# A hybrid decoder layer with a PEER mixer: 96 gathered tokens instead of 64, and the last 32 dense tokens in 32-column strips

## The chip, the cores and the metric

The kernel runs on one core of one Trainium2 chip. The metric is device time in microseconds (us) of one execution, the median of the runs shown; for the kernel before that is 888.08 us (three runs, 887.66 to 889.19). The profile is one execution, recorded by the hardware profiler.

## What is computed

A decoder layer on 256 tokens of width 1024: a mixing part (gated linear attention beside block-sparse attention, one input and one output projection) and then a mixer that looks experts up. Only the mixer is touched by the change. There are 16384 experts, each a row of `peer_u` and a row of `peer_v`; every token picks 128 of them (8 heads, 16 each) by product keys:

```python
    q = (xt @ w_query).reshape(T, PEER_HEADS, 2, PEER_QDIM // 2)
    s = jnp.einsum('thpd,hpkd->thpk', q, subkeys).astype(jnp.float32)
    sv, si = lax.top_k(s, PEER_TOPK)
    ...
    top_s, pos = lax.top_k(cand, PEER_TOPK)
    expert = jnp.take_along_axis(cand_id, pos, axis=-1)
    gate = jax.nn.softmax(top_s, axis=-1)
    ...
        ug = u_tab[ec]
        vg = v_tab[ec]
        act = jax.nn.gelu(jnp.einsum('thkd,td->thk', ug, xc).astype(jnp.float32), approximate=False)
        w = (gc * act).astype(vg.dtype)
        return jnp.einsum('thk,thkd->td', w, vg)
```

## The kernel before

**Two ways for the tokens.** The first `NS` = 64 tokens fetch the rows of their own experts from HBM: a gather (L725, an indirect DMA that GpSimd issues) brings 128 rows of 4 KB, one for each partition. Two partitions serve one token, so 64 gathers of `u_rows` and 64 of `v_rows` cover 64 tokens with 128 experts each. `few_u` (L728) multiplies and sums a gathered tile against the tokens' rows, `few_v` (L737, L740) adds a gathered row, scaled by its gate, into a running sum; both are VectorE instructions over 1024 columns. The gathers have five buffers (L720).

The other `ND` = 192 tokens are computed densely, against all 16384 experts. The *up-projection* (loop at L801, 64 steps `jp` of two 512 KB pieces of `u`) multiplies each piece, in eight f32 matmuls (L112, `by_col_whole`), with the 192 tokens as the moving columns, and applies Gelu. In its second half one-hot matrices of the selected experts (L771, L772, L775) are multiplied in groups of four tokens (L786, 48 groups of eight matmuls) into a grid of gates, which is multiplied into the activations. The *down-projection* (loop at L863) has 128 columns `j` of experts, one 512 KB piece of `v` each. ScalarE and VectorE split the piece (L92, L93) and the weights `W` (L873, L874) into a high and a low part of reduced f32 ("f32r"), so that a product is three f32r matmuls (`mm3`, L68 to L70) instead of one f32 matmul. The result is summed in PSUM over all 128 columns: `prod_a` (L850) for dense tokens 0 to 127, six matmuls of 512 columns for each `j`; `prod_x` (L855) for the other 64, whose high and low weights lie side by side as 128 columns, four matmuls (L859) for each `j`. At the end `few_sum` (L848) and L890 fold partial sums with f32 matmuls of 64 weight columns, L894 adds the residual and L896 stores. In the profile an f32 matmul is two instructions, each with its own weight load; an f32r matmul is one.

**What sets the order.** The program is built with a scheduler (L960, `schedule_with_timeline_sim`): it takes the instructions of the whole kernel and gives each engine one fixed sequence, which may differ from the order of the code. On the chip each engine runs its sequence in order and waits where an operand or a buffer is not ready. Pieces of `u` and `v` pass through five buffers `raw` (L85), loaded by SyncE; the split parts `hi` and `lo` have three each.

Of the kernel before, what the change touches and what calls it, by code (L numbers as in the profile page):

```python
# [13 lines left out]
U32 = mybir.dt.uint32  # L14
# [11 lines left out]
J0 = 30  # L26
NS = 64
# [7 lines left out]
def layer(ctx: ExitStack, tc: tile.TileContext, a):  # L35
# [43 lines left out]
    ready = []  # L79

    def split_next():
# [12 lines left out]
        ready.append((key, k, (hi, lo)))  # L94
# [7 lines left out]
    def by_col(ps, piece, mov, cs=range(NC)):  # L102

        hv, lv = (t.rearrange("p (c f) -> p c f", c=NC) for t in piece)
# [100 lines left out]
    def rows_block(n, engs, after=((), (), (), ())):  # L205
# [3 lines left out]
        for k in range(4):  # L209
            wh, wl = (t.rearrange("p (c f) -> p c f", c=2) for t in take((n, k // 2), k % 2))  # L210
# [294 lines left out]
    ixs = keep.tile([128, 64], U32, name="ixs")  # L505
    gs = keep.tile([128, 64], F32, name="gs")
    hs = keep.tile([128, 64], F32, name="hs")
    rs = keep.tile([128, 1], F32, name="rs")
    two = keep.tile([128, 64], F32, name="two")
    gp.tensor_tensor(two, ident[:, 0:64], ident[:, 64:128], op=OP.add)  # L510
    duo = keep.tile([128, 64], F32, name="duo")
    ident2 = ident.rearrange("p (t m) -> p t m", m=2)
    gp.tensor_tensor(duo, ident2[:, :, 0], ident2[:, :, 1], op=OP.add)
# [15 lines left out]
    yr, accS = ys[:, 0], ys[:, 1]  # L529
# [19 lines left out]
    def rows_of_few():  # L549

        nc.scalar.dma_start(accS, a["n2b"])
        for b in range(2):
            nc.scalar.dma_start(yr[b * 64:(b + 1) * 64], spill[0:NS])
            nc.scalar.dma_start(rs[b * 64:(b + 1) * 64], rstd2[0:NS, 0:1])
        ve.scalar_tensor_tensor(yr, yr, rs, accS, op0=OP.mult, op1=OP.mult)
# [78 lines left out]
    def halves_of(dst, src):  # L634

        for b in range(2):
            nc.scalar.dma_start(dst[b * 64:(b + 1) * 64], src[0:NS, b * 64:(b + 1) * 64])

    def experts():
# [6 lines left out]
        halves_of(ixs, num)  # L646
# [8 lines left out]
    def gates2(tt):  # L655
# [5 lines left out]
        if tt == 0:  # L661
            halves_of(gs, gt.rearrange("p h k -> p (h k)"))
# [57 lines left out]
    gat = ctx.enter_context(tc.tile_pool(name="gat", bufs=5, side="right"))  # L720

# [6 lines left out]
    def few_u(k):  # L728
        g = fetch("u_rows", k)
        junk = gat.tile([128, D], BF, name="junkd", bufs=1)  # L730
        ve.tensor_tensor_reduce(junk, g, yr, 1.0, 0.0, OP.mult, OP.add, hs[:, k:k + 1])  # L731
# [5 lines left out]
    def few_v(k):  # L737
        g = fetch("v_rows", k)
        if k:
            ve.scalar_tensor_tensor(accS, g, hs[:, k:k + 1], accS, op0=OP.mult, op1=OP.add)  # L740
        else:
            ve.tensor_scalar(accS, g, hs[:, 0:1], None, op0=OP.mult)

    few = [lambda k=k: few_u(k) for k in range(64)] + [lambda k=k: few_v(k) for k in range(64)]
    few_done = 0

    def few_to(n):
        nonlocal few_done
        while few_done < min(n, 128):
            if few_done == 64:  # L750
# [50 lines left out]
    for jp in range(64):  # L801
        pv = bank("mm")[:, :2 * ND].rearrange("p (k t) -> p k t", k=2)
        turns, later = later, []
        for k in range(2):
            by_col_whole(pv[:, k], take(("u", jp), k), yf)
# [24 lines left out]
        else:  # L830
            few_to(jp - j1 + 1 if jp < J0 else few_done + (2 if jp % 4 else 1))
# [13 lines left out]
    few0 = few_done  # L845

    def few_sum(p, hf):
        pe.matmul(p[64:128], two, accS[:, hf * 512:(hf + 1) * 512], start=True, stop=True)  # L848

    def prod_a(j, wt, hi, lo):  # L850
        for hf in range(2):
            fs = slice(hf * 512, (hf + 1) * 512)
            mm3(accA[hf], (wt[:, 0:128, 0], wt[:, 0:128, 1]), (hi[:, fs], lo[:, fs]), j == 0, j == NEXP - 1)

    def prod_x(j, wt, hi, lo):  # L855
        for hf in range(2):
            fs = slice(hf * 512, (hf + 1) * 512)
            for m, v in enumerate((hi, lo)):
                pe.matmul(accX[hf], wt[:, 128:ND].rearrange("p t m -> p (t m)"), v[:, fs], start=(j == 0 and m == 0),  # L859
                          stop=(j == NEXP - 1 and m == 1))  # L860

    end = [bank("mm") for _ in range(2)]
    for jp in range(64):  # L863
        if jp == 4:
            nc.sync.dma_start(res[:, 0], spill[NS:NS + 128])
            nc.sync.dma_start(res[0:64, 1], spill[NS + 128:S])
            nc.sync.dma_start(res[64:128, 1], spill[0:NS])
        got = []
        for k in range(2):
            j = 2 * jp + k  # L870
            w = act[j // 64][:, j % 64]
            wt = oh.tile([128, ND, 2], F32R, name="W", tag=("A", "E", "B0", "B1")[j % 4])
            sc_.activation(wt[:, :, 0], w, AF.Copy)  # L873
            ve.tensor_tensor(wt[:, :, 1], w, wt[:, :, 0].bitcast(F32), op=OP.subtract)  # L874
            got.append((j, wt, *take(("v", jp), k)))
# [4 lines left out]
    for hf in range(2):  # L880
        few_sum(end[hf], hf)
    for g in got:
        prod_x(*g)
# [5 lines left out]
    for hf in range(2):  # L889
        pe.matmul(end[hf][0:64], duo, xs[:, hf * 512:(hf + 1) * 512], start=True, stop=True)  # L890
    for b, acc, r0 in ((0, accA, ((0, 128, NS),)), (1, end, ((0, 64, NS + 128), (64, 128, 0)))):
        for hf in range(2):
            fs = slice(hf * 512, (hf + 1) * 512)
            ve.tensor_tensor(res[:, b, fs], res[:, b, fs], acc[hf], op=OP.add)  # L894
            for p0, p1, t0 in r0:
# [68 lines left out]
```

## Time and profile before

| | us |
|---|---|
| median of three runs | 888.08 (887.66 to 889.19) |
| the profiled execution, its own time | 885.1 |
| its span, first to last instruction | 883.2 |
| mixing part, queries and keys, up to the first up-projection matmul | 0 to 197.7 |
| up-projection, with the gate grid | 197.7 to 568 |
| down-projection | 568 to 876 |
| end: last fold, residual, store | 876 to 883.2 |

The stages follow one another on TensorE; the boundaries are the starts and ends of its instruction groups. Times of single instructions in a row overlap with their neighbours, since matmuls are pipelined: the spacing of starts is what one costs.

### The profile page before, as it was taken

Reading aid. Unit: us, or ns where it says so; the run is one execution under the profiler, and the core shown is the slowest. Engines: PE = TensorE matmul, PEld = TensorE weight load, DVE = VectorE, ACT = ScalarE, POOL = GpSimd, SP = SyncE. Lnnn points to the kernel's source line nnn. Section 1 sums busy time; section 2 is a strip of 40 time slices with the busy share of each in tenths; the row PEclk is TensorE's granted clock in tenths of the full one; section 3 lists DMA queues with packets and bytes.
Section 4 is the critical chain, followed back from the end, with each engine's and each line's share of the span. In section 5 each row is a group of like instructions: output and inputs, shape, how many; then the busy total and the mean of one; then the engine's idle time right before and its main releaser. Section 6 shows DMA issues by size and latency. Waiting matters only on the chain.

```text
span 883.2 us, 13836 instructions
## 1 busy us (share of the span) xinstructions
PE 859.7 (97%) x5007; PEld 768.1 (87%) x5007; DVE 615.7 (70%) x1259; ACT 437.6 (50%) x972; POOL 188.0 (21%) x179
## 2 busy tenths in 40 slices
PE   9999999999897999999999999899999999999997
PEld 6876699999896999999999999876888888888885
DVE  4795466799967645456778887888666666666663
ACT  5555355532212600157778776345555555555552
POOL 5131100000024433334445444451000000000000
PEclk9997899999998999999999999999999999999999
DMA  9553027645569999999999999998776767676762
GB/s 344 171 168 105 24 96 265 213 144 170 190 206 360 410 409 409 409 395 355 346 384 365 358 373 364 371 373 310 233 230 228 226 228 234 220 231 223 231 224 64
DMA packets 65875, 235.35 MB, mean 266 GB/s; under 512 B 7936, under 2 KB 8592, under 8 KB 65680
## 3 DMA queue, kind: packets, MB, share of 16 engines
q1 hardware_dynamic: 45696, 164.71, 53.3%
q0 software_dynamic: 18432, 67.12, 20.1%
q10 hardware_dynamic: 1680, 2.65, 1.0%
q8 instruction: 39, 0.64, 0.3%
q14 instruction: 28, 0.23, 0.1%
HBM read 232.29 MB, written 2.10 MB: 265 GB/s over the span
## 4 chain that ended last, share of the span: by engine, by line
PE 86%; DVE 8%; DMA 3%; POOL 1%; issue 1%; ACT 1%; SPq 0%; DVEq 0%; ACTq 0%
PE mm L112 31%; PE sc L859 13%; PE sc L69 7%; PE sc L70 7%; PE sc L68 7%; PE mm L68 4%; PE mm L69 4%; PE mm L70 4%; PE tr L786 3%; DMA rowsof<-in_u_rows,ixs 2%; PE sc L380 1%; DVE lo L93 1%; DVE si L572 1%; DVE junkd L731 1%; PE sc L361 1%
## 5 line engine op out<-in xcount | busy, mean ns | idle before, releaser
L112 PE MATMUL mm<-yf,raw 128*128 128x192 f32 x2048 | 343.8, 328 | 0.0
L112 PEld LDWEIGHTS mm<-yf,raw 128*128 128x128 f32 x2048 | 333.8, 191 | 0.5 <-issue 0.2
L93 DVE TENSOR_TENSOR lo<-raw,hi 128x1024 fp32r<-128x1024 f32 x176 | 215.6, 1227 | 129.2 <-ACT hi L92 129.1
L92 ACT ACTIVATE hi<-raw 128x1024 fp32r<-128x1024 f32 x176 | 185.8, 1058 | 165.8 <-PE sc L70 104.3
L775 ACT ACTIVATE B<-E,gf 128x128 f16<-128x128 f16 x384 | 116.2, 390 | 15.1 <-PE tr L786 11.0
L731 DVE CUSTOM_DVE_ANT_0 junkd<-rowsof,ys 128x1024 bf16<-128x1024 f32 x64 | 78.3, 1223 | 51.7 <-DMA rowsof<-in_u_rows,ixs 42.0
L725 POOL DMA_INDIRECT rowsof<-in_u_rows,ixs x64 | 69.1, 1080 | 189.2 <-PE mm L112 97.3
L725 POOL DMA_INDIRECT rowsof<-in_v_rows,ixs x64 | 87.3, 1364 | 95.0 <-DVE ys L740 66.7
L69 PE MATMUL sc<-lo,W 128*128 128x512 f32 x256 | 101.1, 395 | 1.4 <-DVE lo L93 1.4
L70 PE MATMUL sc<-hi,W 128*128 128x512 f32 x256 | 101.0, 395 | 0.0
L68 PE MATMUL sc<-hi,W 128*128 128x512 f32 x256 | 80.6, 396 | 4.3 <-ACT hi L92 4.3
L740 DVE SCALAR_TENSOR_TENSOR ys<-rowsof,hs,ys 128x1024 f32<-128x1024 f32 x63 | 80.6, 1280 | 0.6
L859 PE MATMUL sc<-lo,W 128*128 128x512 f32 x256 | 80.7, 396 | 0.0
L859 PE MATMUL sc<-hi,W 128*128 128x512 f32 x256 | 80.7, 396 | 0.0
L818 ACT ACTIVATE actA<-mm 128x384 f32<-128x384 f32 x32 | 15.6, 489 | 115.3 <-PE mm L112 106.1
L68 PEld LDWEIGHTS sc<-hi,W 128*128 128x128 f32 x256 | 50.1, 197 | 16.7 <-ACT hi L92 6.3
L69 PEld LDWEIGHTS sc<-lo,W 128*128 128x128 f32 x256 | 50.4, 197 | 14.0 <-DVE lo L93 3.9
L70 PEld LDWEIGHTS sc<-hi,W 128*128 128x128 f32 x256 | 50.3, 197 | 8.7
L859 PEld LDWEIGHTS sc<-lo,W 128*128 128x128 f32 x256 | 48.4, 189 | 10.1
L859 PEld LDWEIGHTS sc<-hi,W 128*128 128x128 f32 x256 | 48.4, 189 | 9.9
L792 DVE SCALAR_TENSOR_TENSOR actA<-tr,actA 128x256 f32<-128x256 f32 x48 | 20.1, 421 | 28.5 <-PE tr L786 20.0
L69 PE MATMUL mm<-qlo,hi 128*128 128x256 f32 x128 | 36.1, 283 | 0.0
(266 smaller groups left out, 1054.1 us busy)
## 6 DMA issues: line engine op xcount, KB each, us to landing
raw<-in_u SPq DMA_DIRECT2D x128, 512.0 KB
raw<-in_v_rows SPq DMA_DIRECT2D x128, 512.0 KB
raw<-in_w_rows SPq DMA_DIRECT2D x20, 512.0 KB
raw<-in_w_q SPq DMA_DIRECT2D x16, 512.0 KB
raw<-in_w_out SPq DMA_DIRECT2D x8, 512.0 KB
raw<-in_w_gqk SPq DMA_DIRECT2D x4, 512.0 KB
xT<-in_xT SPq DMA_DIRECT2D x2, 512.0 KB
xr<-in_x SPq DMA_DIRECT2D x2, 512.0 KB
```

Source lines behind the costliest of these rows:

```text
L68: pe.matmul(ps, sh, mh, start=first, stop=False)
L69: pe.matmul(ps, sh, ml, start=False, stop=False)
L70: pe.matmul(ps, sl, mh, start=False, stop=last)
L92: sc_.activation(hi, raw, AF.Copy)
L93: ve.tensor_tensor(lo, raw, hi.bitcast(F32), op=OP.subtract)
L112: pe.matmul(ps, rv[:, c], mov[:, c], start=(c == 0), stop=(c == NC - 1))
L725: gp.indirect_dma_start(g, None, a[name], bass.IndirectOffsetOnAxis(ap=ixs[:, k:k + 1], axis=0))
L731: ve.tensor_tensor_reduce(junk, g, yr, 1.0, 0.0, OP.mult, OP.add, hs[:, k:k + 1])
L740: ve.scalar_tensor_tensor(accS, g, hs[:, k:k + 1], accS, op0=OP.mult, op1=OP.add)
L775: sc_.activation(B[:, k], E[:, k], AF.Copy, scale=gf[:, m, 4 * q + k:4 * q + k + 1])
L786: pe.matmul(pv[:, k], A[:, k], B[m][:, k], start=(m == 0), stop=(m == 1))
L859: pe.matmul(accX[hf], wt[:, 128:ND].rearrange("p t m -> p (t m)"), v[:, fs], start=(j == 0 and m == 0), stop=(j == NEXP - 1 and m == 1))
```

## The change

- `NS` goes from 64 to 96 and `ND` from 192 to 160. Tokens 64 to 95 use four partitions each, so they need 32 more gathers of `u` and 32 more of `v` (`FEW`): 192 gathers in all instead of 128. Index, gate and row copies are cut up accordingly (six small DMAs each instead of two).
- The gathers are handed to the scheduler at an even pace over the up-projection and the down-projection (`few_to`), and four more buffers (`raw2`) hold pieces of the stream.
- Every fourth column of the down-projection (`whole(j)`) isn't split: `prod_a` uses two f32 matmuls there instead of six f32r ones.
- The other dense tokens of `prod_x` are now 32, in f32 and unsplit. Four columns at a time are collected, and each column's 32 weight columns go to their own strip of the array (`tile_position`), with the strips of PSUM summed at the end by `four`.
- `J0` goes from 30 to 31.

```diff
-J0 = 30
-NS = 64
+J0 = 31
+NS = 96
+FEW = ((0, 64, 2), (64, 32, 4))
+NX = S - NS - 128
...
-        raw = strm.tile([128, 1024], F32, name="raw", bufs=5)
+        n_pieces[0] += 1
+        if gat_raw and n_pieces[0] % 9 >= 5:
+            raw = gat_raw[0].tile([128, 1024], F32, name="raw2", bufs=4)
+        else:
+            raw = strm.tile([128, 1024], F32, name="raw", bufs=5)
         nc.sync.dma_start(raw, src)
-        if key[0] == "u":
-            ready.append((key, k, raw))
+        if key[0] == "u" or key[0] == "v" and whole(2 * key[1] + k):
+            ready.append((key, k, (raw,)))
             return
...
+    def whole(j):
+
+        return j % 4 == 3
...
-    few = [lambda k=k: few_u(k) for k in range(64)] + [lambda k=k: few_v(k) for k in range(64)]
+    few = [lambda k=k: few_u(k) for k in range(NS)] + [lambda k=k: few_v(k) for k in range(NS)]
...
-            few_to(jp - j1 + 1 if jp < J0 else few_done + (2 if jp % 4 else 1))
+            few_to((jp - j1 + 1) * 2 * NS // (64 - j1 + 61))
...
-    def prod_x(j, wt, hi, lo):
-        for hf in range(2):
-            fs = slice(hf * 512, (hf + 1) * 512)
-            for m, v in enumerate((hi, lo)):
-                pe.matmul(accX[hf], wt[:, 128:ND].rearrange("p t m -> p (t m)"), v[:, fs], start=(j == 0 and m == 0),
-                          stop=(j == NEXP - 1 and m == 1))
+    def prod_a(j, w, wt, piece):
+        if wt is None:
+            halved(lambda hf, fs: pe.matmul(accA[hf], w[:, 0:128], piece[0][:, fs], start=False, stop=j == NEXP - 1))
+        else:
+            halved(lambda hf, fs: mm3(accA[hf], (wt[:, 0], wt[:, 1]), (piece[0][:, fs], piece[1][:, fs]), j == 0, False))
+
+    def prod_x(got):
+        def at(hf, fs):
+            for g, (j, w, _, piece) in enumerate(got):
+                pe.matmul(accX[hf][g * NX:(g + 1) * NX], w[:, 128:ND], piece[-1][:, fs], start=j < 4, stop=j >= NEXP - 4,
+                          tile_position=(0, g * NX))
+        halved(at)
...
-            if jp < 63:
+            if j < NEXP - 4:
                 prod_a(*got[-1])
-                prod_x(*got[-1])
-        few_to(few0 + -(-(jp + 1) * (128 - few0) // 61))
...
+            if len(got) == 4 and j < NEXP - 1:
+                prod_x(got)
+                got = []
+        few_to(few_done + -(-(2 * NS - few_done) // max(62 - jp, 1)))
+    assert few_done == 2 * NS
+    prod_x(got)
...
+    def ends(hf, fs):
+        for p0, p1, m, src in ((64, 128, two, ys[:, 0]), (NX, 64, four, ys[:, 1]), (0, NX, four, xs)):
+            pe.matmul(end[hf][p0:p1], m, src[:, fs], start=True, stop=True)
+    halved(ends)
```

**Place one: TensorE's sequence in the middle of the down-projection.** The two numbered banks with the lower numbers are `accA`, the two with the higher are `accX`, for the two halves of 512 result columns. Before, one column `j` of experts:

```order
L68 MATMUL sc_5320<-hi_5821,W_5835 128x512
L68 MATMUL sc_5321<-hi_5821,W_5835 128x512
L859 MATMUL sc_5322<-hi_5821,W_5835 128x512
L859 MATMUL sc_5323<-hi_5821,W_5835 128x512
L69 MATMUL sc_5320<-lo_5822,W_5835 128x512
L70 MATMUL sc_5320<-hi_5821,W_5835 128x512
L69 MATMUL sc_5321<-lo_5822,W_5835 128x512
L70 MATMUL sc_5321<-hi_5821,W_5835 128x512
L859 MATMUL sc_5322<-lo_5822,W_5835 128x512
L859 MATMUL sc_5323<-lo_5822,W_5835 128x512
```

After, from the f32 product of an unsplit column (L871) on; L70 to L72 are the lines of `mm3` and L878 is the strip product:

```order
L871 MATMUL sc_5208<-raw_5886,actA_1390 128x512
L871 MATMUL sc_5209<-raw_5886,actA_1390 128x512
L878 MATMUL sc_5210<-raw_5894,actA_1390 32x512
L878 MATMUL sc_5211<-raw_5894,actA_1390 32x512
L70 MATMUL sc_5208<-hi_5896,W_5916 128x512
L70 MATMUL sc_5209<-hi_5896,W_5916 128x512
L878 MATMUL sc_5210<-raw_5919,actA_1390 32x512
L878 MATMUL sc_5211<-raw_5919,actA_1390 32x512
L71 MATMUL sc_5208<-lo_5897,W_5916 128x512
L72 MATMUL sc_5208<-hi_5896,W_5916 128x512
L71 MATMUL sc_5209<-lo_5897,W_5916 128x512
L72 MATMUL sc_5209<-hi_5896,W_5916 128x512
```

In the code the eight strip products of four columns stand together, the four strips of one half and then those of the other. In the sequence that the scheduler made, each column's two strip products (same piece, same strip, the two halves) stand as a pair between products over all 128 columns. Over the whole stage 256 strip products stand in 115 places: 102 places hold one such pair, 13 hold two pairs of different strips.

**Place two: the end of VectorE's sequence.** L740 before and L757, L759 after are the accumulations of gathered rows of `v`; L93 and L100 are the splits of the stream, L886 and L908 the copy out of `accX`, L894 and L919 the residual. Before, the last five rows:

```order
L874 TENSOR_TENSOR W<-actB,W 128x192
L93 TENSOR_TENSOR lo<-raw,hi 128x1024 x5
L886 COPY xs<-sc 128x512
L894 TENSOR_TENSOR res<-res,sc 128x512 x2
L894 TENSOR_TENSOR res<-res,mm 128x512 x2
```

After, from the split of the last split column on:

```order
L100 TENSOR_TENSOR lo<-raw_7308,hi 128x1024
L908 COPY xs<-sc 128x512
L757 SCALAR_TENSOR_TENSOR ys<-rowsof,hs,ys 128x1024
L919 TENSOR_TENSOR res<-res,sc 128x512
L757 SCALAR_TENSOR_TENSOR ys<-rowsof,hs,ys 128x1024
L919 TENSOR_TENSOR res<-res,sc 128x512
L757 SCALAR_TENSOR_TENSOR ys<-rowsof,hs,ys 128x1024 x15
L759 TENSOR_SCALAR ys<-rowsof,hs 128x1024
L757 SCALAR_TENSOR_TENSOR ys<-rowsof,hs,ys 128x1024 x31
L919 TENSOR_TENSOR res<-res,mm 128x512 x2
```

Before, the last accumulation stands ahead of the 17th split of the 128 in the down-projection. After, 47 of the 96 stand ahead of the last split, 49 behind it, and 47 of these behind the second addition of the residual.

## Rows read from the trace of the kernel before

**Rows 1.** The page: busy time and share of each engine.

```profile
PE 859.7 (97%) x5007; PEld 768.1 (87%) x5007; DVE 615.7 (70%) x1259; ACT 437.6 (50%) x972; POOL 188.0 (21%) x179
```

**Rows 2.** Windows: PE, PEld, DVE, ACT, POOL busy; PE clock, DMA share, GB/s.

```profile
60.00:78.00 18.00, 18.00 (x108) 13.94 (x107) 12.36 (x20) 10.63 (x13) 0.00 (x0) 1.00 0.52 176
...
78.00:96.00 18.00, 18.00 (x59) 9.89 (x60) 4.97 (x19) 7.01 (x24) 2.35 (x1) 0.53 0.09 30
...
189.00:257.00 68.00, 64.86 (x425) 64.48 (x424) 67.66 (x352) 16.13 (x28) 0.00 (x0) 1.00 0.54 179
...
257.00:285.00 28.00, 22.96 (x130) 22.66 (x130) 15.47 (x28) 3.47 (x9) 15.48 (x14) 0.88 0.89 326
...
285.00:420.00 135.00, 133.93 (x885) 132.61 (x884) 77.04 (x143) 50.21 (x160) 53.62 (x51) 1.00 1.01 397
...
568.00:614.00 46.00, 40.24 (x156) 29.71 (x154) 42.19 (x49) 22.34 (x34) 18.18 (x11) 0.96 0.96 355
...
614.00:876.00 262.00, 262.00 (x1133) 217.73 (x1131) 166.35 (x219) 146.17 (x217) 0.00 (x0) 1.00 0.67 217
```

**Rows 3.** The page's groups: up-projection matmuls and DVE accumulates.

```profile
L112 PE MATMUL mm<-yf,raw 128*128 128x192 f32 x2048 | 343.8, 328 | 0.0
...
L740 DVE SCALAR_TENSOR_TENSOR ys<-rowsof,hs,ys 128x1024 f32<-128x1024 f32 x63 | 80.6, 1280 | 0.6
```

**Rows 4.** Chain of waits, up-projection: start, length, what.

```profile
290.92 91.06 PE mm L112 x560
...
381.97 0.89 PE tr L786 x16
```

**Rows 5.** Timeline of PE: 128-column f32 matmuls, then the next ones.

```profile
201.59 1.05 PE L708 MATMUL sc<-skT,qs 128*128 128x128 f32 x8
...
202.48 1.79 PE L112 MATMUL mm<-yf,raw 128*128 128x192 f32 x10
```

**Rows 6.** Chain of waits, down-projection: the same matmul three columns apart.

```profile
630.84 0.47 PE sc L68 x2
...
637.78 0.47 PE sc L68 x2
```

**Rows 7.** Chain of waits around the 64-wide f32 matmuls of L848.

```profile
612.12 0.46 PE sc L859 x2
...
612.58 1.86 PE mm L848 x4
...
614.44 0.67 PE sc L68 x2
```

**Rows 8.** Timeline there: PE's weight loads for L848.

```profile
612.99 0.14 PEld L848 LDWEIGHTS mm<-ys,two 128*64 128x64 f32 x1 [0.29 <-issue]
...
613.42 0.14 PEld L848 LDWEIGHTS mm<-ys,two 128*64 128x64 f32 x1 [0.29 <-issue]
```

**Rows 9.** Timeline of PE: 64-row tiles (L380) and full array (L382) in turn.

```profile
76.10 0.48 PE L380 MATMUL sc<-Tmk,Tmq 64*128 64x128 f32 x2
...
76.52 0.23 PE L382 MATMUL sc<-trib,identb 128*128 128x128 bf16 x1
...
76.68 0.48 PE L380 MATMUL sc<-Tmk,Tmq 64*128 64x128 f32 x2
...
77.10 0.23 PE L382 MATMUL sc<-trib,identb 128*128 128x128 bf16 x1
```

**Rows 10.** Lines L740 and L725: ns min/median/max of one instruction.

```profile
L740 DVE SCALAR_TENSOR_TENSOR ys<-rowsof,hs,ys x63: 1274/1279/1286, 435.2 to 610.5; 128x1024 f32<-128x1024 f32 x63
...
L725 POOL DMA_INDIRECT rowsof<-in_u_rows,ixs x64: 932/936/2415, 257.1 to 417.1; - x64
```

**Rows 11.** Chain of waits, the kernel's end.

```profile
876.05 1.88 PE mm L890 x4
...
877.95 0.69 DVE res L894
```

**Rows 12.** Waits of PE: waiter, releaser, us in total, times, longest.

```profile
PE tr L630 <- DVE ij L625: 8.2, 2, 5.0
```

More of the change, by code (lines that the diff above doesn't have):

```diff
@@ L209, in rows_block @@
         for k in range(4):
-            wh, wl = (t.rearrange("p (c f) -> p c f", c=2) for t in take((n, k // 2), k % 2))
+            wh, wl = (t.rearrange("p (c f) -> p c f", c=2) for t in take((n, k // 2), k % 2)[:2])
             for tt in range(NT):
@@ L503, in layer @@
     gf = keep.tile([128, 2, ND], F32, name="gf")
[L505 to L508, printed above, removed]
+    ixs = keep.tile([128, NS], U32, name="ixs")
+    gs = keep.tile([128, NS], F32, name="gs")
+    hs = keep.tile([128, NS], F32, name="hs")
+    rs = keep.tile([128, 2], F32, name="rs")
     two = keep.tile([128, 64], F32, name="two")
     gp.tensor_tensor(two, ident[:, 0:64], ident[:, 64:128], op=OP.add)
-    duo = keep.tile([128, 64], F32, name="duo")
-    ident2 = ident.rearrange("p (t m) -> p t m", m=2)
-    gp.tensor_tensor(duo, ident2[:, :, 0], ident2[:, :, 1], op=OP.add)
+    four = keep.tile([128, 32], F32, name="four")
+    gp.tensor_tensor(four, two[:, 0:32], two[:, 32:64], op=OP.add)
+    sums = (two, four)
     tk_ctx = ExitStack()
@@ L748, in few_to @@
         nonlocal few_done
[L749 to L750 removed]
+        while few_done < min(n, 2 * NS):
+            if few_done == NS:
                 few_gates()
@@ L871, in layer @@
             w = act[j // 64][:, j % 64]
[L872 to L875, printed above, removed]
-            if jp < 63:
-                prod_a(*got[-1])
-                prod_x(*got[-1])
-        few_to(few0 + -(-(jp + 1) * (128 - few0) // 61))
[L880 to L883, printed above, removed]
+            wt = None
+            if not whole(j):
+                wt = oh.tile([128, 2, 128], F32R, name="W", tag=("A", "E", "B0", "B1")[j % 4])
+                sc_.activation(wt[:, 0], w[:, 0:128], AF.Copy)
+                ve.tensor_tensor(wt[:, 1], w[:, 0:128], wt[:, 0].bitcast(F32), op=OP.subtract)
+            got.append((j, w, wt, take(("v", jp), k)))
+            if j < NEXP - 4:
+                prod_a(*got[-1])
+            if len(got) == 4 and j < NEXP - 1:
+                prod_x(got)
+                got = []
+        few_to(few_done + -(-(2 * NS - few_done) // max(62 - jp, 1)))
+    assert few_done == 2 * NS
+    prod_x(got)
     xs = oh.tile([128, D], F32, name="xs", tag="gl", bufs=1)
@@ L888, in layer @@
         prod_a(*g)
-    for hf in range(2):
-        pe.matmul(end[hf][0:64], duo, xs[:, hf * 512:(hf + 1) * 512], start=True, stop=True)
-    for b, acc, r0 in ((0, accA, ((0, 128, NS),)), (1, end, ((0, 64, NS + 128), (64, 128, 0)))):
+    def ends(hf, fs):
+        for p0, p1, m, src in ((64, 128, two, ys[:, 0]), (NX, 64, four, ys[:, 1]), (0, NX, four, xs)):
+            pe.matmul(end[hf][p0:p1], m, src[:, fs], start=True, stop=True)
+    halved(ends)
+    for b, acc in enumerate((accA, end)):
         for hf in range(2):
@@ L894, in layer @@
             ve.tensor_tensor(res[:, b, fs], res[:, b, fs], acc[hf], op=OP.add)
-            for p0, p1, t0 in r0:
+            for p0, p1, t0 in rows_at[1:] if b else rows_at[:1]:
                 nc.sync.dma_start(a["out"][t0:t0 + p1 - p0, fs], res[p0:p1, b, fs])
```

57 lines of the change are left out of this document (30 added, 27 removed).

## The prediction, made before the run

> **What bounds the kernel now.** The page's first part comes first: TensorE (PE) is busy for 859.7 of 883.2 us and no other engine for more than 70% [rows 1]. The windows say where that holds: in the up-projection (285 to 420) PE works 133.9 of 135 us, in the down-projection (614 to 876) 262 of 262 [rows 2]. Only three spots wait for something else: 68 us of top-k in which VectorE is busy 67.7 us and PE waits 8.2 us for transposes [rows 2, 12], the same work's end at 257 to 285, and the down-projection's first columns (40.2 of 46 us). So in these two stages a change is worth what it does to PE's sum of matmuls, and to what remains after PE's last one. The profiled execution took 885.1 us, 3.0 less than the median of 888.08; I sum against 885.1 and add 3.0 at the end.
>
> **Prices on PE.** The up-projection's f32 matmul over 192 columns is two instructions; 560 instructions in 91.06 us are 0.1626 us each [rows 4]. Over 128 columns eight instructions start 0.89 us ahead of the next group, 0.111 each [rows 5]. For 160 columns I interpolate: 0.137. In the down-projection the same matmul stands 6.94 us apart over three columns of ten f32r matmuls each, 0.2313 us for one [rows 6]. An f32 matmul over 512 columns is two instructions 0.43 us apart [rows 8]; so one f32 matmul costs 0.86, nearly four f32r ones. L848 shows what a pair of such matmuls on part of the array costs between products over the whole array: 1.86 us for its four instructions, and the next two f32r matmuls take 0.67 instead of 0.47 [rows 6, 7]: 1.86 + 0.20 = **2.06 us a pair**, of which 4 x 0.43 = 1.72 is streaming and 0.34 the two changes between part and whole. A second place gives the same: L380 on 64 rows (two instructions over 128 columns, 2 x 0.107 by their columns at the full clock) and L382 over 128 columns at bf16 (0.05) together take 0.58 a turn, 0.31 more than they stream [rows 9].
>
> **The change part by part.**
>
> *Up-projection.* 2048 matmul instructions [rows 3], each 0.1626 - 0.137 = 0.0256 cheaper: **-52.4**. The grid loses 8 of 48 groups, 64 matmuls of 0.89 / 16 = 0.0556 [rows 4]: **-3.6**. Top-k is VectorE's and stays as long; in TensorE's new sequence its transposes stand behind more matmuls, so that the waits [rows 12] neither grow nor go by more than some 5 us: I take 0. The loads must keep up: two pieces of 0.524 MB in a step of 32 x 0.137 + 1.25 x 0.445 = 4.94 us are 212 GB/s, and by VectorE's sequence some 75 gathers (0.524 MB each) fall into the 240 us that are left of this stage, 164 GB/s; 376 together, under the 397 that the window 285 to 420 reached without PE waiting [rows 2]. The extra index and gate DMAs are issued by ScalarE, which has room here (50 of 135 us). If that cover fails it costs some 10 us.
>
> *Down-projection.* Before: 1280 f32r matmuls of 0.2313 and one L848 place, 296.1 + 2.1 = 298.2. After:
> - 96 split columns, six f32r matmuls each: 576 x 0.2313 = 133.2;
> - 32 unsplit columns, two f32 matmuls of two instructions: 128 x 0.43 = 55.0;
> - the strips. The code writes them so that four strips could run side by side, but the sequence (place one) holds a column's two halves as a pair, in the same strip, and then products over the whole array. The second of a pair needs the same 32 columns as the first and the next product needs all, so nothing is left to run beside it. No row shows a 32-wide strip; the nearest is L848, 64 wide, at 2.06 a pair, and a narrower one streams the same 512 columns. 102 places x 2.06 + 13 places x (2.06 + 1.72) = 210.1 + 49.1 = 259.2. Bounds: 218.6 (streaming alone, 512 x 0.427) and 66 (four truly at once, 32 x 2.06), which is the first rival.
>
> Sum 447.4, so **+149.2**. VectorE has less to do per column than PE now: per four columns three splits and three W, about 4.7 us, and two or three accumulations of 1.28, against 14 us of PE. ScalarE likewise. The first columns' waits of 5.8 us [rows 2] shrink, as each column takes PE longer: **-4**.
>
> *End.* Before, 7.15 us lie between the last product (876.05) and the end of the span [rows 11]. After, VectorE's sequence (place two) has 47 accumulations behind the second residual addition, which waits for PE's last product over all columns; they can't be done earlier, whoever is idle, and the last fold waits for them. One costs 1.28 us on VectorE [rows 3, 10]; GpSimd issues one in 0.94 and about 0.3 of gap; the transfer takes 0.524 MB / 397 GB/s = 1.32 [rows 2], and no load stands beside it now. Five buffers let the three overlap, so I take 1.33: 62.5 us. From above, the gathers of 285 to 420 came one in 135 / 51 = 2.65 us, beside the stream [rows 2]. Around them stand two residual additions and one accumulation (about 1.5 after PE's end), four f32 folds of 0.94 (four instructions, so two folds, in 1.88 [rows 11]), an addition and the store (0.69 + 4.55): some 9.0. In all 73, **+66**.
>
> *Sum.* 885.1 - 52.4 - 3.6 + 149.2 - 4 + 66 = 1040; with 3.0 to the median, **1043 us**, 17% slower.
>
> **The rivals.**
>
> *The strips do run four at once* (the change does what it says), because the chip starts a strip while products ahead of it still run in other strips. Then the strips cost 66 instead of 259.2 and the kernel takes 1043 - 193 = 850, faster by 4%. For it speaks that the strips are independent in code; against it the sequence, and that in rows 7 the full-width product behind L848 came late, not early. It decides from strips of 104 us in all, 0.81 a column: below that the change gains, since 52 + 4 + 4 of gain and 298 of old products stand against 66 of end, 133 and 55. By a rule of the Trainium skill (TensorE: Matmul & The Clock Gate, measured speedup vs the span model) three column strips side by side ran 2.38 times as fast as one after another; as an estimate by that page 259 / 2.38 = 109 would make it 893, about no change. No run here has strips side by side.
>
> *The clock falls.* In the stretch 78 to 96, where L380 and L382 and other tiles of part of the array take turns, PE counts as busy all the time and yet the granted clock is 0.53, that is mostly the lower of its two levels, 1.2 GHz; in 60 to 78, whose end has the same turns, it was 1.00, the upper, 2.4 GHz [rows 2, 9]. If the turns of strips and whole array in the down-projection bring this about, its 447 us become up to 850 (every product twice as long): 1143 if a quarter of the stage is hit, 1445 for all. Against it: at L848's place the four instructions kept 0.43 [rows 8], the price of the upper level, and here a strip pair is followed by long products again.
>
> *The end's gathers are slow*, as they were beside the stream: 47 x (2.65 - 1.33) = 62 more, 1105. For it speaks that GpSimd's issues stretch to 2.4 us at times [rows 10]; against it that the stream was what they shared the DMA with.
>
> *The changes between strip and whole array are free* for 32-wide tiles: 115 x 0.34 = 39 less, 1004.
>
> **How the numbers follow.** The forecast with its two bounds (slow gathers, free changes) has 0.80: its own range is 1003 to 1105. The falling clock has 0.10, all of it slower. The strips at once, wholly or enough to gain, have 0.09; landing by chance within 0.2%, about what a measurement of this kernel can tell from no change, 0.01. Faster 0.09, same 0.01, slower 0.90. The range from 990 to 1110 holds the forecast with both bounds and leaves out the two far cases.
>
> **What would show it.** In the profile after: the up-projection's matmuls about 0.137 us apart and that stage some 56 us shorter; the strip products' line with 512 instructions and about 0.43 us between the two of a matmul, the stage near 447 us; the granted clock at 1.0 through it; then some 62 us in which PE is idle and VectorE and GpSimd alternate on L757 and gathers, in the last slices of the page. Wrong would be: strip instructions of different columns with starts a few ns apart, a down-projection under 300 us, or accumulations that end before PE does.

## The result

The kernel after the change takes 1023.5 us (median of six executions) against 888.6 for the kernel before beside it: a ratio of 1.150, 95% interval 1.146 to 1.155. It is slower by 15%. The prediction was 1043, with 990 to 1110 as its range. One of the six took 1603.7 us, with a mean granted clock of TensorE of 0.55; the ratio leaves it out.

The profiled execution took 1018.26 us with a span of 1016.5. Three points split the span: the first product of the down-projection, the end of its last one, and the end of the span.

| us | before | after | change | predicted |
|---|---|---|---|---|
| down-projection begins | 569.8 | 505.5 | -64.3 | -56.0 |
| its length | 306.3 | 423.5 | +117.2 | +145.2 |
| from its end to the end of the span | 7.2 | 87.5 | +80.3 | +66 |
| span | 883.2 | 1016.5 | +133.3 | +155 |

The sign, the stages and their order are as predicted; each size is off by 8 to 28 us.

The page's first part of the kernel after, as in [rows 1]:

```profile
PE 925.5 (91%) x4883; PEld 627.6 (62%) x4883; DVE 630.4 (62%) x1269; ACT 361.9 (36%) x835; POOL 261.1 (26%) x243
```

The windows of the kernel after, with the columns of [rows 2]; the last two rows are the new down-projection and the new end:

```profile
189.00:257.00 68.00, 65.49 (x493) 64.56 (x491) 67.76 (x363) 16.46 (x26) 0.09 (x1) 1.00 0.71 232
257.00:285.00 28.00, 27.47 (x201) 27.34 (x202) 15.76 (x26) 3.98 (x12) 13.74 (x13) 1.00 0.99 375
285.00:420.00 135.00, 133.75 (x1068) 132.82 (x1067) 72.31 (x153) 68.24 (x235) 39.78 (x39) 1.00 1.00 387
506.00:929.00 423.00, 422.89 (x1215) 164.53 (x1214) 223.33 (x288) 118.24 (x187) 91.56 (x74) 1.00 0.72 243
930.00:1007.00 77.00, 3.25 (x4) 0.75 (x4) 60.22 (x49) 0.00 (x0) 55.40 (x43) 0.54 0.88 306
```

In the up-projection PE works 133.8 of 135 us as before and does 1068 instructions there in place of 885; the loads keep up at 387 GB/s. In the down-projection it is busy for 422.9 of 423 us at a granted clock of 1.00, the upper level, and DMA is used for only 0.72. Then come 77 us in which PE does next to nothing.

The new up-projection's price, in the chain of waits (start, length, what), beside [rows 4]; and PE's wait for the transposes, beside [rows 12]:

```profile
312.56 41.56 PE mm L123 x304
```

```profile
PE tr L643 <- DVE ij L638: 1.2, 1, 1.2
```

41.56 / 304 = 0.1367 us an instruction, where 0.137 was interpolated. The wait of 8.2 us has become 1.2.

The strip products in the timeline of PE (start, length, engine, line, operation, count), first a pair alone, then a place where the pairs of two columns follow each other:

```profile
627.43 0.40 PE L72 MATMUL sc<-hi,W 128*128 128x512 f32 x1
627.75 1.90 PE L878 MATMUL sc<-raw,actA 128*32 128x512 f32 x4
629.59 0.73 PE L70 MATMUL sc<-hi,W 128*128 128x512 f32 x2
630.15 0.40 PE L71 MATMUL sc<-lo,W 128*128 128x512 f32 x1
```

```profile
560.16 1.92 PE L878 MATMUL sc<-raw,actA 128*32 128x512 f32 x8
562.01 0.74 PE L70 MATMUL sc<-hi,W 128*128 128x512 f32 x2
```

This is the row to learn from. Four instructions (one column, both halves, one strip) take 1.90 us, and eight (two columns, two strips) take 1.92: **the second column is free.** Alone, a pair keeps PE from 627.66 (the f32r product before it has had its 0.23) to 629.59, and the next two products take 0.10 more than their 0.46 (629.59 to 630.15): 2.03. So the rival of the prediction, strips that run at once, is right wherever strips meet; it is the sequence that lets them meet at 13 of 115 places only.

The end, all engines, in the timeline:

```profile
966.70 1.67 POOL L741 DMA_INDIRECT rowsof<-in_v_rows,ixs  x1 [0.30 <-issue]
968.29 1.28 DVE L757 SCALAR_TENSOR_TENSOR ys<-rowsof,hs,ys 128x1024 f32<-128x1024 f32 x1 [0.73 <-DMA rowsof<-in_v_rows,ixs]
968.68 1.71 POOL L741 DMA_INDIRECT rowsof<-in_v_rows,ixs  x1 [0.30 <-issue]
970.17 3.98 DVE L757 SCALAR_TENSOR_TENSOR ys<-rowsof,hs,ys 128x1024 f32<-128x1024 f32 x3 [0.59 <-DMA rowsof<-in_v_rows,ixs]
```

A sum is 1.28 as in [rows 10], but VectorE waits between sums for a gather, and GpSimd's issue takes up to 1.71 there (1.29 in the mean at this end), not 0.94.

### The profile page after: what moved, and what is told of

Read it like the earlier page. It is cut to its first block, busy times and chain, and to the rows that moved or that the text cites. A ratio compares the mean times of both kernels' runs of the same rounds, so it can differ in the third digit from the quotient of the medians.

```text
span 1016.5 us, 13628 instructions
## 1 busy us (share of the span) xinstructions
PE 925.5 (91%) x4883; PEld 627.6 (62%) x4883; DVE 630.4 (62%) x1269; ACT 361.9 (36%) x835; POOL 261.1 (26%) x243
## 4 chain that ended last, share of the span: by engine, by line
PE 36%; issue 34%; POOL 11%; DVE 9%; DMA 7%; ACT 1%; ACTq 1%; SPq 0%; POOLq 0%; DVEq 0%
PE mm L123 21%; POOL rowsof L741 11%; PE mm L70 3%; PE mm L71 3%; PE mm L72 3%; DMA rowsof<-in_v_rows,ixs 2%; PE tr L803 2%; DMA raw<-in_u 1%; DMA raw<-in_v_rows 1%; DVE lo L100 1%; PE sc L391 1%; DVE si L585 1%; DMA ys<-x_rows 1%; ACT B L792 1%; DVE scs L583 1%
## 5 line engine op out<-in xcount | busy, mean ns | idle before, releaser
L123 PE MATMUL mm<-yf,raw 128*128 128x160 f32 x2048 | 288.1, 300 | 2.1 <-ACT actA L835 1.2
L123 PEld LDWEIGHTS mm<-yf,raw 128*128 128x128 f32 x2048 | 279.6, 190 | 2.9 <-ACT actA L835 1.7
L100 DVE TENSOR_TENSOR lo<-raw,hi 128x1024 fp32r<-128x1024 f32 x144 | 173.8, 1222 | 65.3 <-ACT hi L99 65.3
L741 POOL DMA_INDIRECT rowsof<-in_u_rows,ixs x96 | 103.6, 1079 | 358.6 <-DVE hs L747 247.0
L741 POOL DMA_INDIRECT rowsof<-in_v_rows,ixs x96 | 122.2, 1273 | 257.0 <-DVE ys L757 215.2
L757 DVE SCALAR_TENSOR_TENSOR ys<-rowsof,hs,ys 128x1024 f32<-128x1024 f32 x94 | 120.5, 1282 | 16.8 <-DMA rowsof<-in_v_rows,ixs 15.6
L878 PE MATMUL sc<-raw,actB 128*32 128x512 f32 x256 | 110.5, 598 | 0.0
L878 PE MATMUL sc<-raw,actA 128*32 128x512 f32 x256 | 108.6, 598 | 0.0
L792 ACT ACTIVATE B<-E,gf 128x128 f16<-128x128 f16 x320 | 96.3, 387 | 13.3 <-PE tr L803 10.6
L71 PE MATMUL sc<-lo,W 128*128 128x512 f32 x192 | 81.5, 424 | 0.1
L72 PE MATMUL sc<-hi,W 128*128 128x512 f32 x192 | 75.9, 395 | 0.0
L71 PEld LDWEIGHTS sc<-lo,W 128*128 128x128 f32 x192 | 36.0, 187 | 51.3 <-issue 22.6
L70 PE MATMUL sc<-hi,W 128*128 128x512 f32 x192 | 67.0, 430 | 0.0
L70 PEld LDWEIGHTS sc<-hi,W 128*128 128x128 f32 x192 | 31.2, 188 | 54.9 <-issue 31.0
L878 PEld LDWEIGHTS sc<-raw,actB 128*32 128x32 f32 x256 | 21.0, 109 | 64.4 <-issue 64.4
L878 PEld LDWEIGHTS sc<-raw,actA 128*32 128x32 f32 x256 | 20.6, 109 | 63.0 <-issue 62.2
```

Source lines behind the costliest of these rows:

```text
L70: pe.matmul(ps, sh, mh, start=first, stop=False)
L71: pe.matmul(ps, sh, ml, start=False, stop=False)
L72: pe.matmul(ps, sl, mh, start=False, stop=last)
L123: pe.matmul(ps, rv[:, c], mov[:, c], start=(c == 0), stop=(c == NC - 1))
L741: gp.indirect_dma_start(g, None, a[name], bass.IndirectOffsetOnAxis(ap=ixs[:, k:k + 1], axis=0))
L757: ve.scalar_tensor_tensor(sumS, g, hs[:, k:k + 1], sumS, op0=OP.mult, op1=OP.add)
```

## The experiments

Theories at the start: (A) a strip product that stands beside other strips costs nothing, and the loss in the down-projection is the sequence that puts 102 pairs alone; (B) strips run one after the other wherever they stand. For the end: (C) a queue that the order of VectorE makes, or (D) transfers that have no other place.

**Four strips together.** TensorE's order is tied so that the 8 strip products of four columns stand together:

```diff
+        with tc.issue_after(last[0].ins):
+            halved(at)
...
     def prod_a(j, w, wt, piece):
+        with tc.issue_after(last[0].ins) if last[0] else nullcontext():
+            prods_a(j, w, wt, piece)
```

> All of the change is kept; only the order on TensorE is fixed so that the 8 strip products of four columns (four strips of the first half, then four of the second) stand directly together, after the whole-array products of the fourth column and before those of the next. Theory (strips that stand beside other strips run at the same time; the change lost time because its strip products were queued as pairs of one strip between whole-array products): a set of 8 takes about 2.1 us in place of four pairs at about 2.0 each, the down-projection's TensorE work is 576 x 0.2313 + 32 x 1.81 + 32 x 2.1 = 258 us; the loads and gathers that fall into it (128 + about 95 of 512 KB at 1.3 us) then set its length, about 290 us; about 32 gathers are left for the end at 1.6 us. Time about 855 us (835 to 880). Rival (the strips of a group run one after the other): 133 + 58 + 32 x (4 x 1.83 + 0.34) = 436 us for the stage, time 1015 to 1031 us. Half-way rival (two strips at a time): about 905 us.

Measured: 878.9 us, ratio to before 0.991 (0.988 to 0.994): at the upper end of the theory's range, 145 us faster than the change and a little faster than the kernel before. Its timeline of PE, a whole set of four columns:

```profile
646.58 1.88 PE L877 MATMUL sc<-raw,actA 128*128 128x512 f32 x4
648.39 1.92 PE L885 MATMUL sc<-raw,actA 128*32 128x512 f32 x16
650.25 0.73 PE L70 MATMUL sc<-hi,W 128*128 128x512 f32 x2
```

Sixteen instructions in 1.92 us; B falls. The stage shrinks from 423.5 to 318.7, not to 290, for PE now waits, and the window of the stage shows DMA full (columns as in [rows 2]):

```profile
PE sc L71 <- DVE lo L100: 20.2, 35, 1.1
PE sc L70 <- ACT hi L99: 16.1, 12, 1.3
```

```profile
511.00:829.00 318.00, 281.37 (x1221) 143.79 (x1219) 254.22 (x312) 119.67 (x187) 133.85 (x98) 0.98 0.96 362
```

Some of the splits that PE waits for wait themselves for pieces (ScalarE 18.5 us in this window): 0.96 of DMA at 362 GB/s. The end shrinks from 87.5 to 45.9, since the scheduler's new sequence for VectorE has more sums ahead of the last product.

**Every column split.** One line, and all 128 pairs stand alone:

```diff
     def whole(j):
-        return j % 4 == 3
+        return False
```

> The change with every column split, none unsplit; the strips stay. In the order of TensorE all 128 pairs of strip products then stand alone between whole-array products. Theory (an isolated pair costs about 2.06 us whoever stands around it, and VectorE has 32 more columns to split): the down-projection is 768 x 0.2313 + 128 x 2.06 = 441 us in place of 424, and some 53 sums rather than 47 are left for the end: about 1018 + 17 + 6 x 1.63 = 1045 us (1035 to 1062). Rival (an unsplit column costs 1.81 us in place of 6 x 0.2313 = 1.39, so splitting them again gains 32 x 0.42 = 13 us): about 1005 us.

Measured: 1043.9 us. The stage goes from 509.7 to 950.4, 440.7 us where 441 was expected. That settles the price of a pair alone: (440.7 - 768 x 0.2313) / 128 = 2.06 us. An unsplit column, 4 x 0.43 = 1.72 in place of 6 x 0.2313 = 1.39, is dearer by itself and yet pays in the change: all 13 places where two pairs meet stand right behind such a column, as at 560.16 above. (The 1.81 us from 646.58 to 648.39 hold 0.09 for the change to the strips, as much as a pair takes behind an f32r product, 627.66 to 627.75.)

**Sums at an even pace.** VectorE's order is tied so that the split of each column's weights follows a set number of sums:

```diff
+    def few_by(jp):
+        return min(2 * NS, 62 + jp * (2 * NS - 62) // 60)
...
+                with tc.issue_after(few_ins[few_by(jp) - 1].ins):
+                    ve.tensor_tensor(wt[:, 1], w[:, 0:128], wt[:, 0].bitcast(F32), op=OP.subtract)
...
-        few_to(few_done + -(-(2 * NS - few_done) // max(62 - jp, 1)))
+        few_to(few_by(jp + 1))
```

> All of the change is kept; VectorE's order is fixed so that the sums over gathered rows of the down-projection are done at an even pace within it (two more per two columns) rather than 47 of them behind the last product. Theory (the end is a queue of sums that nothing hides, 1.63 us each, and the stage has DMA time and VectorE time to spare, 128 loads + 127 gathers x 1.3 us = 332 of its 423 us): about 10 sums are left behind the last product, 37 x 1.63 = 60 us go, time about 958 us (945 to 975). Rival (the gathers take the loads' DMA time, or the sums hold up the splits that TensorE waits for): what leaves the end comes back in the stage, time 1005 to 1025 us.

Measured: 883.0 us, ratio 0.995 (0.993 to 0.998); 75 us less than expected. The end went as expected and more (87.5 to 4.5). What I missed is the stage, 423.5 to 365.6: the tie on VectorE made the scheduler order TensorE anew, so that only 31 pairs stand alone and nearly all others in sets of two to four columns. One of three columns:

```profile
815.15 0.61 PE L71 MATMUL sc<-lo,W 128*128 128x512 f32 x2
815.70 1.93 PE L879 MATMUL sc<-raw,actB 128*32 128x512 f32 x12
817.56 0.73 PE L72 MATMUL sc<-hi,W 128*128 128x512 f32 x2
```

So this run changed two things, and speaks for C (the end's queue was order) but can't price it alone.

**Only the first part: 96 tokens.** The strips and the unsplit columns go; the last 32 dense tokens' products are f32r with both parts side by side, as before:

```diff
-                pe.matmul(accX[hf][g * NX:(g + 1) * NX], w[:, 128:ND], piece[-1][:, fs], start=j < 4, stop=j >= NEXP - 4,
-                          tile_position=(0, g * NX))
+                for m in range(2):
+                    pe.matmul(accX[hf][0:2 * NX], wt[:, 128:ND].rearrange('p t m -> p (t m)'), piece[m][:, fs], start=j == 0 and m == 0,
+                              stop=j == NEXP - 1 and m == 1)
```

> Only the first part of the change: 96 gathered tokens. The last 32 dense tokens' products of the down-projection are done as before, split in two and side by side (64 columns, every column split, none unsplit, no strips). Theory (the strips and the unsplit columns cost about 115 us in the down-projection): it takes 1280 x 0.2313 = 296 us and some waits, 300 to 310 as in the kernel before; about 54 sums are left for the end; time about 506 + 305 + 54 x 1.63 + 12 = 911 us (895 to 925). Rival (the strips cost little and the stage is long because of the extra gathers beside it): 990 to 1020 us.

Measured: 906.5 us, ratio 1.021 (1.015 to 1.026), as expected. The stage takes 300.5 us, so that the strips and the unsplit columns, in the places where the change has them, cost 423.5 - 300.5 = 123. Against the kernel before, the 96 tokens alone give 56 us in the up-projection and 6 in the down-projection and take 87 at the end (94.4 in place of 7.2).

**Short sums at the end.** 32 of 1024 elements of each sum, the gathers all made:

```diff
-            ve.scalar_tensor_tensor(sumS, g, hs[:, k:k + 1], sumS, op0=OP.mult, op1=OP.add)
+            ve.scalar_tensor_tensor(sumS[:, 0:32], g[:, 0:32], hs[:, k:k + 1], sumS[:, 0:32], op0=OP.mult, op1=OP.add)
```

> The change with the sums over gathered rows of the down-projection cut to 32 of 1024 elements each (the rest of the sums is left out); the gathers are all made. Theory A (each gather of the end costs its own transfer and issue, 1.6 us, whatever VectorE does): the end stays near 87 us and the time near 1018 us. Theory B (VectorE's 1.28 us sum is in the chain, and holds up GpSimd's issue beside it): a gather costs 1.0 to 1.3 us, the end is 15 to 30 us shorter, time 988 to 1003 us.

Measured: 1012.5 us (one run), between the two. Its up-projection ended 9 us later, so the end is read by itself: 72.8 us in place of 87.5, at the edge of what B says. Windows of GpSimd's line L741 (busy, count, clock, DMA share, GB/s) and that line's group between 930 and 1007 (busy, mean ns), the two of the change first, then the two with short sums:

```profile
932.00:1000.00 68.00, 53.33 (x41) 0.53 0.90 316
```

```profile
L741 POOL DMA_INDIRECT rowsof<-in_v_rows,ixs x43 | 55.4, 1288 | 16.7 <-issue 9.8 <-DVE ys L757 5.1 <-DMA rowsof<-in_v_rows,ixs 1.8
```

```profile
940.00:996.00 56.00, 37.03 (x41) 0.54 0.99 377
```

```profile
L741 POOL DMA_INDIRECT rowsof<-in_v_rows,ixs x44 | 41.3, 939 | 36.5 <-DVE ys L757 28.3 <-issue 7.4 <-DVE ys L759 0.8
```

41 gathers in 68 us are 1.66 each, in 56 us 1.37. Beside short sums an issue takes 0.94 in place of 1.29, and the DMA engines fill up (0.99 in place of 0.90). So 1.37 is the transfer's, as predicted (1.33), and 0.29 comes with the long sums: beside VectorE's instruction over 1024 columns, with two inputs from SBUF, GpSimd's issue is longer. The Trainium skill (GPSIMD Engine Reference, section Specifications) says that GpSimd's way to SBUF is shared with VectorE and contended by just such instructions; the two rows agree with it.

**Both corrections**, the two ties above in one kernel:

> Both corrections of order at once: four strips together on TensorE, and the sums over gathered rows at an even pace in the down-projection. Theory (with either correction alone the DMA engines are already the bound: 0.95 to 1.0 of them busy in the down-projection at 362 to 405 GB/s; 35 gathers that move from the end into the stage lengthen it by 35 x 1.3 to 1.45 us, as much as they saved): about 876 us (865 to 885), no better than either alone. Rival (the two gains add: the end's 35 sums go and the stage stays at 319 us): 511 + 319 + 8 = 838 us (830 to 850).

Measured: 879.2 us, ratio 0.993 (0.990 to 0.996), as either alone. The window of its down-projection:

```profile
514.00:868.00 354.00, 291.48 (x1222) 147.23 (x1221) 276.27 (x335) 119.65 (x187) 156.55 (x117) 0.93 0.94 356
```

The end is 8.2 us and the stage 355.3 in place of 318.7: what left the end came back, as D says. But the longest wait of PE in it is for VectorE's split of the weights (L910), which the tie puts behind the sums, and GpSimd waits for VectorE in its turn before it issues gathers:

```profile
PE sc L72 <- DVE W L910: 47.3, 22, 6.9
POOL rowsof L741 <- DVE W L910: 75.2, 31, 7.7
```

So DMA at 0.94 and an order that the tie made stand side by side here, and this run by itself doesn't say which of them sets the time.

**96 tokens, no strips, sums paced**, the first part with the same tie on VectorE:

> Only 96 gathered tokens, the last 32 dense tokens split in two as before (no strips, no unsplit column), and the sums at an even pace in the down-projection. Theory (DMA is the bound of the stage whatever TensorE does in it): 128 + 122 transfers of 512 KB at 1.3 to 1.45 us = 325 to 362 us, time about 508 + 350 + 8 = 866 to 880 us, the same as with strips within 15 us. Rival (TensorE's 296 us is the bound): 508 + 300 + 8 = 816 us. Second rival (VectorE: 128 x 1.22 + 128 x 0.35 + 122 x 1.28 = 357 us and its waits): 880 to 900 us.

Measured: 883.9 us, ratio 0.997 (0.9943 to 0.9995): just above the theory's range and in the second rival's, which the run doesn't tell apart (VectorE is busy for 323 of the stage's 362 us, DMA for 0.92). The first rival falls: with 296 us of products where the strips need 258, the time is 5 us behind the run before.

**Every column unsplit, strips together**: no splits at all in the stage, and the tie on TensorE as above, not the one on VectorE (the code also spreads its sums over two steps fewer).

```diff
     def whole(j):
-        return j % 4 == 3
+        return True
```

> Four strips together, and every column of the down-projection unsplit: no splits by ScalarE and VectorE there, TensorE's work is 128 x 1.81 + 32 x 1.86 = 291 us. Theory (transfers are the bound): 255 of them at 1.3 to 1.4 us = 332 to 357 us, up-projection to 508 and 5 us behind: about 860 us (845 to 875), a little under 879 since no transfer waits for a split. Rival (waits for the splits are what holds the stage at 0.95 of DMA): TensorE's 291 us and some sums behind it, about 830 us (815 to 840).

Measured: 877.7 us, ratio 0.990 (0.987 to 0.993), 3 us above the theory's range, and the rival falls. That is the time of the run with four strips together (878.9), though VectorE, without its splits, is busy for only 114 of 250 us in the window 520 to 770. DMA is full there at 406 GB/s and PE waits for the loads themselves; then the sums that are left follow (the stage 316.9, the end 46.6). This kernel with its sums paced wasn't run.

```profile
520.00:770.00 250.00, 232.27 (x787) 80.15 (x784) 113.77 (x111) 0.28 (x1) 84.74 (x90) 1.00 1.03 406
```

```profile
PE sc L877 <- DMA raw<-in_v_rows: 17.6, 43, 0.7
```

**Pace from the up-projection on.** The same tie, in the second half of the up-projection too:

```diff
+    def held():
+        return tc.issue_after(few_ins[few_done - 7].ins) if few_done > 6 else nullcontext()
...
-            grid_group(done_q, 2 * jp + 2)
+            with held():
+                grid_group(done_q, 2 * jp + 2)
```

> As the two corrections together, and VectorE's order is fixed in the second half of the up-projection too, so that 86 rather than 65 of the gathered rows are used before the down-projection begins. Theory (DMA is 0.98 to 0.99 busy in the up-projection already, so 21 more gathers there push the loads of TensorE's data back by 21 x 1.4 = 29 us and save as much later): the same time as without it, within 10 us. Rival (370 GB/s is not the limit, 405 are to be had): 21 x 1.3 = 27 us less.

Measured: 867.9 us in three runs (860.0 to 870.5) and 878.7 in a fourth, which the ratio of 0.976 (0.970 to 0.983) leaves out. That is some 11 us less than without the tie, at the edge of what the theory allows and well short of the rival's 27; with runs so far apart the size of the gain is uncertain. It is the fastest of the kernels that compute everything, about 2.4% ahead of the kernel before. That a mere change of VectorE's order gains again speaks against transfers alone setting the time of the two corrections together.

**Take the transfers away.** The first attempt let each gather fetch 64 partitions in place of 128, and each sum read 64, so that half of the rows are missing:

```diff
-        gp.indirect_dma_start(g, None, a[name], bass.IndirectOffsetOnAxis(ap=ixs[:, k:k + 1], axis=0))
+        gp.indirect_dma_start(g[0:64], None, a[name], bass.IndirectOffsetOnAxis(ap=ixs[0:64, k:k + 1], axis=0))
```

> As the two corrections together (879 us), with each gather and its sum on 64 of 128 partitions: half of the gathered rows, 50 MB, are neither fetched nor summed. Theory (DMA is the bound of that kernel): 192 x 0.65 to 0.7 us of DMA time go, about 125 to 135 us, more than is needed to hand the bound back to TensorE: up-projection to about 508, 258 us of products in the down-projection with some 15 us of waits, 8 us after it: about 790 us (780 to 805). Rival (it is the waits on splits and sums, VectorE's order, that hold the stage): 860 to 880 us, since VectorE's instructions keep their number and length.

Measured: 902.3 us (one run); both numbers missed. The page's part on DMA queues (packets, MB, share of 16 engines' span; q1 carries the loads, q0 the gathers), with both corrections and whole gathers first (span 876.9), then with half gathers (span 900.4):

```profile
q1 hardware_dynamic: 45744, 164.71, 51.1%
q0 software_dynamic: 27648, 100.68, 30.8%
```

```profile
q1 hardware_dynamic: 45744, 164.71, 59.0%
q0 software_dynamic: 15360, 50.34, 23.0%
```

Half of the bytes still take 207 of 270 us (23.0% of 900.4, 30.8% of 876.9), and the loads, unchanged in bytes, take 531 us in place of 448. So this edit didn't take away what it was to take away, and says nothing for or against the theory. The Trainium skill (DMA: Bandwidth & Descriptors, section The descriptor swizzle) says that in a transfer to all partitions engines 0 to 7 write partitions 0 to 63 and engines 8 to 15 the others; that would load half of the engines with every row of these gathers. No row here tells engines apart, and all 16 together show 1.04 (window 285 to 420), so why the loads suffered stays open.

The second attempt leaves out every second gather, on all partitions, and keeps all sums (the odd ones read the row tile before):

```diff
     def fetch(name, k):
+        if k % 2:
+            return held_rows[0]
         g = gat.tile([128, D], F32, name="rowsof", tag="rowsof")
```

> As the two corrections together (879 us), with every second gather left out: its sum reads the row tile that the gather before it brought, on all 128 partitions. All sums stay, 96 of 192 transfers of 512 KB go. Theory (transfers are the bound of that kernel): up-projection to about 506, 258 us of products with some 15 us of waits, 8 us behind: about 790 us (780 to 810). Rival (VectorE's order and the splits that TensorE waits for are the bound, since VectorE keeps all its instructions): 855 to 880 us.

Measured: 785.2 us (one run), against 879.2 with them. The window of its down-projection, 504.7 to 775.6:

```profile
504.00:770.00 266.00, 258.53 (x1212) 141.16 (x1211) 199.37 (x248) 118.53 (x185) 48.07 (x25) 0.99 0.80 294
```

PE is the bound again, 258.5 of 266 us at 0.80 of DMA. VectorE does as much as before in the whole kernel (620 us against 623), but not in the same order: 125 sums stand ahead of its first split of the weights in place of 65, 57 rather than 94 of those over rows of `v` fall into the stage, and PE's 47.3 us of waiting for that split are gone. So it is shown that with 96 tokens and PE's sequence put right the 96 transfers are worth 94 us. Whether they cost it as loads that come late, or as sums that come late with their gathers and hold up the splits, this run doesn't say; the run without splits speaks for the loads, the pace from the up-projection on for a part of the order.

**Between the two: 80 tokens.** 16 more tokens gathered eight slots at once, the last 48 as before in f32r, the sums paced, and without the four extra buffers `raw2`:

```diff
-NS = 96
-FEW = ((0, 64, 2), (64, 32, 4))
+NS = 80
+FEW = ((0, 64, 2), (64, 16, 8))
```

> Between the two kernels: 80 gathered tokens (the last 16 of them eight slots at once), the last 48 dense tokens split in two and side by side as before (96 columns), no strips, no unsplit column, sums ahead of the end. Theory (64 tokens are bound by TensorE at 885, 96 by DMA at about 880): TensorE's up-projection is shorter than before by half of what it is with 96, about 26 us, the down-projection is as before, 128 + 128 + 160 transfers in place of 448 are 32 x 1.4 = 45 us less than with 96: the larger of 859 (TensorE) and 835 (DMA), about 858 us (848 to 868). Rival (the two bounds do not hide each other and add in part): 870 to 885 us.

Measured: 892.2 us, ratio 1.007 (1.004 to 1.009), worse than both bounds and than the rival. The down-projection begins at 562.5, only 7 us earlier than before, and takes 319.6, 13 more. Of the first I can name one wait, of PE for ScalarE's one-hot factors (L792) where the up-projection's second half begins. ScalarE waits there for VectorE's one-hot matrix (L788), which stands in VectorE's order behind sums that each wait for a gather. The second goes with a VectorE that is busy 84 of 86 us (614 to 700):

```profile
PE tr L803 <- ACT B L792: 12.7, 1, 12.7
ACT B L792 <- DVE E L788: 15.2, 1, 15.2
```

```profile
293.25 1.23 DVE L746 CUSTOM_DVE_ANT_0 junkd<-rowsof,ys 128x1024 bf16<-128x1024 f32 x1 [1.32 <-DMA rowsof<-in_u_rows,ixs]
```

```profile
614.00:700.00 86.00, 86.00 (x330) 56.59 (x329) 84.00 (x99) 43.12 (x66) 45.14 (x27) 1.00 0.99 377
```

That the gathers' denser pace in this order causes both is a guess, and what the missing buffers cost was not tried.

## Why the prediction was right, and where its sizes were off

- **Up-projection, -52.4 and grid -3.6.** Right: 0.1367 an instruction against 0.137. The stage came out another 8 us shorter, 7.0 of them PE's wait for transposes, which I had left at 8.2 and which is 1.2 now; the prediction says that they stand behind more matmuls in the new sequence, allowed some 5 us either way, 2 too few, and drew no gain from it. The loads kept up, with 387 GB/s where 376 were reckoned.
- **The sequence decides, not the code.** Right, and shown from both sides: with all pairs alone (every column split) the stage is 441, with sets of four 319. The latter is bounded by transfers as well, so it doesn't give the strips' price alone.
- **A pair alone, 2.06, and an unsplit column, 4 x 0.43.** Right, both: the first, from a tile twice as wide, is 2.06 over 128 pairs; the second is 1.72, and 0.09 more where strips follow, which the pair's price holds already.
- **13 places at 2.06 + 1.72.** This step failed. I let two pairs side by side cost two pairs; they are different strips and take 1.85 together (560.16 to 562.01), with 0.19 for the changes ahead and behind some 2.04. 13 x (3.78 - 2.04) = 23 of the 28 us by which the stage was oversized. About 4 more are waits: the forecast left half of the 8 us that the stage had before, and PE is now busy for 422.9 of 423.
- **"Nothing is left to run beside it."** Right for a pair between whole-array products, and the reason why the first rival (four at once, 850) didn't come about: it was put at 0.09 on the sequence. With the sequence mended the strips do cost about 66 (16 instructions in 1.92, with the changes around them 2.06, 32 times), and yet the kernel takes 879, not 850: PE then waits, with DMA at 0.96. The rival's sum had left out the loads' and gathers' share of a shorter stage. For three strips side by side the Trainium skill (TensorE: Matmul & The Clock Gate, measured speedup vs the span model) has 2.38 times; here three columns take 1.93 us against 1.90 for one, 2.95 times, so the measurement is the one to use for f32 over 512 columns.
- **The clock.** It stayed at 1.00 through the down-projection (506 to 929), as argued; that rival fell for the profiled run. One of its figures is also wrong: twice 447 is 894, not 850, so its two cases come to 1155 and 1490.
- **The end, 47 sums at 1.33.** The mechanism was right (VectorE and GpSimd in turn on L757 and L741, PE idle), the size low: 1.66 apiece, 47 x 0.33 = 16, where the end exceeds the forecast by 14. The transfer was sized rightly (1.37 with short sums); that the issue is longer beside the sums (1.29 in place of 0.94) was not in it; a sum keeps its 1.28. The slow bound of 2.65 was not reached.
- **Sum.** 1040 against 1018 for the profiled execution: 28 too long in the down-projection, 8 in the up-projection, and 14 too short at the end, which cancels in part: that the total came nearer (22) than the down-projection alone is luck.

## What to carry to other kernels

Products on a part of the array are only cheap in company: read from the engine's actual sequence, not from the code, whether neighbours lie in different strips, and tie them together if a scheduler may pull them apart. When work moves from an engine to gathers, add up the transfers of the stage as well as the engine's instructions: here every kernel with 96 tokens, all its gathers whole and its strips or sums put in order lands between 868 and 884, with DMA at 0.92 or more in its down-projection, and without half of the 192 gathers it takes 785. And work that "is spread to the end" lies behind the end if the scheduler so orders it; the tail's price is the count of what stands behind the last product times the slowest of its links.

## What the runs showed of the hardware that I had not expected

- One to four 32-column strips of f32 products over 512 columns take the same time: 1.90, 1.92, 1.93 and 1.92 us for 4, 8, 12 and 16 instructions. They need not write or read the same tiles: at the end two folds with different inputs start together (timeline of the kernel after).

```profile
1007.29 1.06 PE L914 MATMUL mm<-ys,four 128*32 128x512 f32 x1 [49.65 <-DVE ys L757]
1007.29 1.06 PE L914 MATMUL mm<-xs,four 128*32 128x512 f32 x1
```

- GpSimd's issue of a gather takes 0.94 us in the mean beside sums over 32 elements, and 1.29 beside sums over 1024.
- Gathers onto 64 of 128 partitions took 0.77 of the DMA time of whole ones (207 of 270 us), and the loads beside them 531 us in place of 448.
